# Two transfers on GpSimd's queue instead of six on ScalarE's, and half of the output weights loaded behind a store

## The chip, the cores and the metric

The kernel runs on one core of a Trainium2 chip. A core has TensorE (PE) for matmuls, VectorE (DVE), ScalarE (ACT), GpSimd (POOL) and SyncE (SP), which here does nothing but request transfers. All engines run at once and wait for each other by semaphores. ScalarE and GpSimd can request transfers as well; a request stands in that engine's own instruction stream, so what comes behind it waits until it is issued. The metric is device time in microseconds of one execution: the median of several runs.

## The reference

One encoder layer is applied to two sequences, a prompt of 256 positions and a sample of 2048, with 1024 features each:

```python
h = rms_norm(x, g_pre)
q, k, v, z_a, u_f, z_f = split(h @ w_in)                # each 512 wide
y_a = neighbourhood_attention(q, k, v, rpb)             # 8 heads of 64, windows of 8 x 16 on a grid 64 wide
spec = jnp.fft.fft2(u_f as [s, 8, 64], axes=(s, 64), norm='ortho')
y_f = spec.real.reshape(s, 512) @ w_f + b_f             # a Fourier mix, then a dense product
mixed = concat([rms_norm(y_a, g_na) * silu(z_a), rms_norm(y_f, g_f) * silu(z_f)])
out = x + rms_norm(mixed @ w_out, g_post)
```

Everything is float32 from input to output. The kernel keeps that precision by splitting each operand of the large products into a rounded high part and a remainder (`h`, `l`) and summing three products (`mm3`, lines 160 to 162).

## The kernel before

The work runs in four stretches on TensorE.

First (0 to about 549 us) come the six input projections, with the sums of a fast matrix scheme made by VectorE and GpSimd. The results go to memory outside the core: `qD`, `kD`, `vD`, `zD` and, for the Fourier half, `ZD` (first stage of the transform over positions). In the same stretch the output weights are scaled and split, and stored as `woD` (`wo_split`, line 704).

Second (549 to 576 us) comes the second stage of the Fourier transform. It loops over four groups `gq` and five blocks of features `c` (`stage2`, line 1031). Each block's product lands in a PSUM tile (`pab`; in group 0 also `pny`, in group 2 also `pup` for the prompt), and ScalarE's rounded copy (`split_ps`, line 1012) and VectorE's difference (line 1013) put the parts into `abh`, `abl`. Block 4 holds one feature per group of 64, the thirty-third: a real transform over 64 features has 33 distinct terms, and the last of them has no room in the four full blocks. It is kept in `a32`, three copies of 32 partitions each: rounded, rounded, remainder.

Between groups, `pq` (line 1052) multiplies the cosine and sine tables `cs2` by the dense weights `wf`. It runs with `m = 1` behind group 1 and with `m = 0` behind group 2. For `m = 1`, every thirty-second row of the product belongs to that thirty-third feature. It is copied out (`nq_`), and four rows of each `c` are moved to the rows they have in `w32`, the partner of `a32`: partitions 0 to 31 rounded, 32 to 63 remainder, 64 to 95 rounded. One matmul of 96 rows (line 1265) thus does all three products of that feature. The moving across partitions is done by transfers through the zeroed tile `nw`: three on ScalarE's queue for each `c`, one to each copy. Then one ScalarE copy of 96 partitions and one VectorE subtraction on the middle 32 finish `w32`.

Third (576 to 613 us), for each of four blocks `e` of 128 output features, three column tiles `ti` (in the order 2, 0, 1) are multiplied (`y_mm`, line 1254) into PSUM tiles `py1` (ring "a") and `py2` (ring "b", two tiles), and put together (`y_out`, line 1268): ScalarE writes `t1` from `py1` with the bias, VectorE adds or subtracts `py2` into `Y`. `Y` has two buffers; block `e` writes the buffer of block `e - 2`. When a block is done its 256 prompt positions are stored (line 1304) and then its 2048 sample positions, 1 MB (line 1327). For the first blocks ScalarE and GpSimd also sum the squares of Y (lines 1333 to 1341). The first output tile needs rows of all four blocks back from memory as `y0` (lines 1323, 1324, 1326), multiplied by `z` and split (lines 1350 to 1354).

Fourth (613 us to the end) come attention, in 36 groups, with the Fourier half of the output product (`f_mm`, line 1444, weights `wo1`) between them, and then the attention half.

`wo1` is eight tiles of 512 KB: `wo1[n][c]` for two halves `n` of the output columns and four blocks `c` of inner features. All eight are loaded in one loop (lines 1234 to 1237) on SP, behind the first loads of q, v, z and tables for attention. The half `n = 0` is first used by `f_mm(0)` and `n = 1` by `f_mm(1)`, the first and the second product of the fourth stretch. The tiles come from the pool of `gt`, whose buffers the second stretch used for `zg` and `d2`.

What sets the order of the work: TensorE's order is that of the code throughout. Of the other engines it is so up to line 972 and from line 1343, where `e` is 3. Between these lines, so in all that the diff touches, a planner orders ScalarE, VectorE, GpSimd and SP ahead of time by its own estimates: what stands first in the code goes first unless it is reckoned to be not ready, and then something later may go ahead. Once made, the order is fixed, and on the chip each engine's queue waits at its head.

Of the kernel before, what the change touches and what calls it, by code (L numbers as in the profile page):

```python
# [10 lines left out]
F32 = mybir.dt.float32  # L11
F32R = mybir.dt.float32r
AF = mybir.ActivationFunctionType
ALU = mybir.AluOpType
# [150 lines left out]
def build(tc, A, O):  # L165
    nc = tc.nc
# [60 lines left out]
    def gt(shape, dtype, name):  # L227
        return gp.tile(shape, dtype, tag="g", name=name)
# [485 lines left out]
    for c in range(3, 6):  # L714
# [7 lines left out]
        if c == 4:  # L722
# [5 lines left out]
            for k in range(KC):  # L728
                for t in range(2):
                    ts = slice(128 * t, 128 * t + 128)  # L730
                    nc.vector.scalar_tensor_tensor(out=xp[:, k, ts], in0=xs[t][:, k], scalar=gpre[:, k:k + 1],
                                                   in1=ivb[0][:, ts], op0=ALU.mult, op1=ALU.mult)
# [257 lines left out]
    sm = pg.enter_context(tc.tile_pool(name="smF", bufs=1))  # L990
# [1 line left out]
    nc.sync.dma_start(cs2, A["cs"])  # L992
    wf = sm.tile([128, 4, 512], F32, name="wf")
    nc.sync.dma_start(wf, A["wf"])
    nw = sm.tile([96, 512], F32, name="nw")
    nc.gpsimd.memset(nw, 0.0)
    f256 = sm.tile([128, 2, 258], F32, name="f256")
    nc.sync.dma_start(f256, A["f256"])
# [12 lines left out]
    def split_ps(dh, dl, src, vec=False):  # L1011
        nc.vector.tensor_copy(dh, src) if vec else nc.scalar.copy(dh, src)
        nc.vector.tensor_tensor(out=dl, in0=src, in1=dh.bitcast(F32), op=ALU.subtract)
# [36 lines left out]
    w32 = ab.tile([96, 512], F32R, name="w32")  # L1050

    def pq(m):
        h = gt([128, 2, 512], F32R, "pqh")
        l = gt([128, 2, 512], F32R, "pql")
        for c in range(2):
            p = ps.tile([128, 512], F32, tag="a", name="ppq")
            for x in range(2):
                nc.tensor.matmul(p[64 * x:64 * x + 64], cs2[:, m, :], wf[:, 2 * c + x, :], start=True, stop=True)
            if m == 0:
                split_ps(h[:, c], l[:, c], p)  # L1060
                continue
            nq_ = sm.tile([128, 512], F32, name="nq", bufs=2)
            nc.scalar.copy(nq_, p)
            for r in range(3):
                nc.scalar.dma_start(nw[32 * r + 16 * c:32 * r + 16 * c + 16:4], nq_[::32])
            nc.scalar.activation(h[:, c], p, AF.Copy, scale=dnyq[:, 2:3])
            nc.vector.scalar_tensor_tensor(out=l[:, c], in0=p, scalar=dnyq[:, 2:3], in1=h[:, c].bitcast(F32),
                                           op0=ALU.mult, op1=ALU.subtract)
        PQ[m] = h, l
        if m:  # L1070
            nc.scalar.copy(w32, nw)
            nc.vector.tensor_tensor(out=w32[32:64], in0=nw[32:64], in1=w32[32:64].bitcast(F32), op=ALU.subtract)

    for gq in range(4):
        for c in range(5):
            stage2(gq, zgs[gq], c)
        if gq in (1, 2):
            pq(2 - gq)
# [45 lines left out]
    def prep(g):  # L1124
        pr, ts = g["pr"], g["ts"]
        g["qh"] = jl.tile([128, 256], F32R, tag="qh", name="qh", bufs=4)
        g["ql"] = jl.tile([128, 256], F32R, tag="ql", name="ql", bufs=4)
        if g["R"] is None:
            q = qD[pr, :, ts].rearrange("p (b x) -> p b x", b=2)
        else:  # L1130
            sg, x = divmod(g["R"], 2)
            t0 = TP + 1024 * sg + 512 * g["hc"]
            q = qD[pr, :, t0:t0 + 512].rearrange("p (b x) -> p b x", b=2)[:, :, 128 * x:128 * x + 128]
        nc.sync.dma_start(g["ql"].bitcast(F32).rearrange("p (b x) -> p b x", b=2), q)
# [25 lines left out]
    def split_q(g):  # L1160
        qh, ql = g["qh"], g["ql"]
        nc.scalar.copy(qh, ql.bitcast(F32))
        nc.gpsimd.tensor_tensor(out=ql, in0=ql.bitcast(F32), in1=qh.bitcast(F32), op=ALU.subtract)
# [48 lines left out]
    def soft(g, b):  # L1212
        m = g["m"][b]
        nc.vector.reciprocal(m[:, 4:6], m[:, 2:4])  # L1214
        for h in range(2):
            w = g["w"][b][:, h, :g["nr"] * g["t"][b][1]]
            nc.gpsimd.tensor_scalar(w, w, m[:, 4 + h:5 + h], 1.0, ALU.mult, ALU.mult)  # L1217
# [13 lines left out]
        prep_v(g)  # L1231
    load_t(0, 1)
    wo1 = [[gt([128, 2, 512], F32R, "wo1") for c in range(4)] for n in range(2)]
    for n in range(2):
        for c in range(4):
            nc.sync.dma_start(wo1[n][c].bitcast(F32),
                              woD[1, :, c, :, n * 512:n * 512 + 512].rearrange("x p d -> p x d"))
    prep(G[2])
    prep(G[3])
    for g in G[:2]:  # L1240
# [2 lines left out]
    sm = pg.enter_context(tc.tile_pool(name="smY", bufs=2))  # L1243
    sqy = pq_.enter_context(tc.tile_pool(name="sqy", bufs=1, side="right"))
    y0 = sqy.tile([128, 2, 4, 128], F32, name="y0")
    for t, (g, x) in enumerate(zip(G, (0, 640))):
        g["w"] = []
        for c0, w in g["t"]:
            n = 2 * g["nr"] * w
# [4 lines left out]
    def y_mm(e, ti):  # L1254
        n = 386 if ti == 2 else 384
        cs = slice(384 * ti, 384 * ti + n)
        p1 = ps.tile([128, 512], F32, tag="a", name="py1")
        p2 = ps.tile([128, 512], F32, tag="b", name="py2", bufs=2)
        es_ = slice(e * 128, e * 128 + 128)
        for m, p in ((0, p1), (1, p2)):  # L1260
            for c in range(2):
                mm3(nc, p[:, :n], PQ[m][0][:, c, es_], PQ[m][1][:, c, es_],
                    AB[m][0][:, c, cs], AB[m][1][:, c, cs], c == 0, m == 1 and c == 1)
            if m == int(e == 0 and ti == 2):
                nc.tensor.matmul(p1[:, :n], w32[:, es_], a32[:, cs], start=False, stop=True)
        return p1, p2, n
# [39 lines left out]
    def first_soft(g, f=None):  # L1306
        if f:
            for y in range(4):
                bias_max(g, *divmod(y, 2))
            f()  # L1310
        for y in range(4):
            if f is None:
                bias_max(g, *divmod(y, 2))
            exps(g, *divmod(y, 2))

    order = ExitStack()
    for e in range(4):
        Y = sqy.tile([128, T], F32, tag="Y", name="Y", bufs=2)
        if e < 3:
            for ti in (2, 0, 1):  # L1320
                y_out(e, ti, *y_mm(e, ti))
                if e == 2 and ti == 2:
                    nc.sync.dma_start(y0[:, 0, :3], yD[1, :3, :, :128].rearrange("c p t -> p c t"))
                    nc.sync.dma_start(y0[:, 1], zD[0, :, :128].rearrange("(c p) t -> p c t", p=128))
                if e == 2 and ti == 0:
                    nc.gpsimd.tensor_tensor(out=y0[:, 0, :3], in0=y0[:, 0, :3], in1=y0[:, 1, :3], op=ALU.mult)
            nc.sync.dma_start(yD[1, e, :, TP:], Y[:, TP:])
            if e == 2:
                Y2 = Y
            for i in range(T // SQ if e < 2 else 1):  # L1330
                ts = slice(i * SQ, i * SQ + SQ)
                if e == 0:
                    nc.scalar.activation(sqs[:, ts], Y[:, ts], AF.Square)
                elif e == 2:
                    sq = sm.tile([128, SQ], F32, tag="sqf", name="sqf", bufs=2)
                    nc.scalar.activation(sq[:, :TP], Y[:, :TP], AF.Square)
                    nc.gpsimd.tensor_tensor(out=sqs[:, :TP], in0=sqs[:, :TP], in1=sq[:, :TP], op=ALU.add)
                else:
                    sq = sm.tile([128, SQ], F32, tag="sqf", name="sqf", bufs=2)
                    nc.scalar.activation(sq, Y[:, ts], AF.Square)  # L1340
                    nc.gpsimd.tensor_tensor(out=sqs[:, ts], in0=sqs[:, ts], in1=sq, op=ALU.add)
            continue
        order.enter_context(tc.manual_schedule(engines=MAN))
        py = y_mm(e, 2)
        scores(G[0])
        first_soft(G[0], lambda: y_out(e, 2, *py))
        py = y_mm(e, 0)
        y0h = gt([128, 2, 4, 128], F32R, "y0h")
        y0h = [y0h[:, 0], y0h[:, 1]]
        nc.vector.tensor_tensor(out=y0[:, 0, 3], in0=Y[:, :128], in1=y0[:, 1, 3], op=ALU.mult)  # L1350
        sq = sm.tile([128, SQ], F32, tag="sqf", name="sqf", bufs=2)
        y_out(e, 0, *py, lambda: (nc.scalar.copy(y0h[0], y0[:, 0]),
                                  nc.scalar.activation(sq[:, :TP], Y[:, :TP], AF.Square)))
        nc.vector.tensor_tensor(out=y0h[1], in0=y0[:, 0], in1=y0h[0].bitcast(F32), op=ALU.subtract)
        soft(G[0], 0)
        soft(G[0], 1)

        nc.sync.dma_start(y0[:, 0], yD[1, :, :, 128:256].rearrange("c p t -> p c t"))
        nc.sync.dma_start(y0[:, 1], zD[0, :, 128:256].rearrange("(c p) t -> p c t", p=128))
        scores(G[1])  # L1360
        py = y_mm(e, 1)
        first_soft(G[1])
        nc.vector.tensor_tensor(out=sqs[:, :TP], in0=sqs[:, :TP], in1=sq[:, :TP], op=ALU.add)
        split_q(G[2])
        soft(G[1], 0)
        y_out(e, 1, *py)
# [6 lines left out]
    sm = pt.enter_context(tc.tile_pool(name="smA", bufs=2))  # L1373
# [412 lines left out]
```

## Time and profile before

| | |
|---|---|
| median of three runs | 972.06 us (969.88, 972.06, 975.32) |
| the profiled execution | 973.49 us, of which the span from the first to the last instruction is 971.4 us |
| mean granted clock of TensorE | 0.996 |
| TensorE busy | 957.9 us, 99% of the span |
| VectorE, ScalarE, GpSimd busy | 710.4, 497.0, 430.3 us |
| moved by transfers | 279.22 MB, 287 GB/s on average |

In the rows that follow, a line of a timeline gives the start and the duration in microseconds, the engine, the line of the kernel, the operation, the tile written and the tile read, the shape and how many instructions are merged into the row. A bracket at the end gives the idle time of that engine just before, and what ended it. SPq and ACTq are the streams of requested transfers of SP and ScalarE; their duration is that of the request with its wait in the queue, not of the transfer. Tile names are cut of their numbers: `w` with `nw` beside it is `w32`, `wo` from `woD` is `wo1`.

### The profile page before, as it was taken

What the parts mean: (1) busy time and instruction counts of PE and PEld (TensorE: products, weight loads), DVE (VectorE), ACT (ScalarE), POOL (GpSimd) and SP (SyncE); (2) the same over time, 40 slices, a digit from 0 to 9 for tenths busy, and PEclk for the clock granted to TensorE, in tenths of its full rate; (3) what the DMA queues carried; (4) which work ended last, traced back from release to release, by engine and by line L of the source; (5) the groups of instructions that cost most, each with busy time, mean ns of one, the idle gap of its engine ahead of it and who ended that gap; (6) DMA issues with size and microseconds to landing.
All of it is one profiled execution on the core that took longest, in us unless ns stands there. A gap on an engine that the chain in (4) does not pass through costs nothing. (4 is left out here: it accounts for less than half of the span.)

```text
span 971.4 us, 17021 instructions
## 1 busy us (share of the span) xinstructions
PE 957.9 (99%) x5737; PEld 799.2 (82%) x5737; DVE 710.4 (73%) x1306; ACT 497.0 (51%) x1080; POOL 430.3 (44%) x401
## 2 busy tenths in 40 slices
PE   9999999999999999999999999999999999999997
PEld 7889988888888888888888878888787888778886
DVE  6768988777986767797776454776765656649997
ACT  5836675433325533333344255677666676644443
POOL 3100003364752202756745033577677686524544
PEclk9999999999999999999999999999999999999999
DMA  9899696556849996599889897698877998979993
GB/s 333 306 373 356 235 364 239 193 193 258 318 157 381 347 408 240 210 374 331 304 301 335 303 307 298 188 284 288 264 230 235 288 296 279 287 250 340 339 340 127
DMA packets 146286, 279.22 MB, mean 287 GB/s; under 512 B 13738, under 2 KB 84096, under 8 KB 142808
## 3 DMA queue, kind: packets, MB, share of 16 engines
q1 hardware_dynamic: 145720, 277.69, 81.8%
q8 instruction: 46, 0.75, 0.3%
q10 hardware_dynamic: 480, 0.44, 0.2%
q14 instruction: 40, 0.33, 0.1%
HBM read 183.66 MB, written 101.52 MB: 294 GB/s over the span
## 5 line engine op out<-in xcount | busy, mean ns | idle before, releaser
L160 PE MATMUL mm<-xh,wa 128*128 128x512 f32 x448 | 174.4, 389 | 0.0
L161 PE MATMUL mm<-xl,wa 128*128 128x512 f32 x448 | 174.3, 389 | 0.0
L162 PE MATMUL mm<-xh,wa 128*128 128x512 f32 x448 | 174.3, 389 | 0.0
L532 POOL TENSOR_TENSOR ws<-wr 128x512 f32<-128x512 f32 x16 | 22.5, 1406 | 227.7 <-DMA wr<-wz 209.8
L1217 POOL TENSOR_SCALAR w<-w,m 128x465 f32<-128x465 f32 (+9 forms) x136 | 85.6, 643 | 43.6 <-DVE m L1214 33.5
L160 PEld LDWEIGHTS mm<-xh,wa 128*128 128x128 f32 x448 | 84.1, 188 | 17.7
L162 PEld LDWEIGHTS mm<-xh,wa 128*128 128x128 f32 x448 | 84.1, 188 | 17.5
L161 PEld LDWEIGHTS mm<-xl,wa 128*128 128x128 f32 x448 | 84.1, 188 | 17.3
L547 DVE TENSOR_TENSOR wa<-wr,wa 128x512 fp32r<-128x512 f32 x60 | 71.9, 1207 | 26.8 <-ACT wa L546 26.6
L1434 PE MATMUL po<-wo,yh 128*128 128x512 f32 x272 | 90.5, 414 | 0.0
L1434 PE MATMUL po<-w,yh 128*128 128x512 f32 x280 | 86.9, 391 | 0.0
L1210 ACT ACTIVATE w<-w,m 128x465 f32<-128x465 f32 (+9 forms) x136 | 78.3, 579 | 16.5 <-DVE m L1205 16.4
L1205 DVE CUSTOM_DVE_ANT_1 w<-s,tb 128x465 f32<-128x465 f32 (+8 forms) x124 | 61.2, 532 | 10.2 <-PE s L1183 9.3
L585 POOL TENSOR_TENSOR mt<-mt,rmask 128x880 f32<-128x880 f32 (+2 forms) x24 | 50.6, 2124 | 34.4 <-DVE mt L581 21.1
L161 PE MATMUL mm<-vl,xh 128*128 128x512 f32 x168 | 65.6, 390 | 0.2 <-DVE vl L478 0.2
L162 PE MATMUL mm<-vh,xl 128*128 128x512 f32 x168 | 65.4, 389 | 0.0
L160 PE MATMUL mm<-vh,xh 128*128 128x512 f32 x168 | 65.4, 389 | 0.0
L873 DVE TENSOR_TENSOR f<-u,mm 128x512 f32<-128x512 f32 x64 | 43.5, 679 | 26.2 <-PE mm L162 21.3
L1434 PEld LDWEIGHTS po<-w,yh 128*128 128x128 f32 x280 | 52.1, 188 | 11.2 <-issue 0.4
L546 ACT CAST wa<-wr 128x512 fp32r<-128x512 f32 x60 | 36.3, 617 | 44.5 <-PE mm L162 23.0
L1507 PE MATMUL ptb<-ident,w 128*120 128x128 f32 (+8 forms) x422 | 58.9, 277 | 0.1
L1511 DVE COPY pt<-ptb 120x384 f32<-120x384 f32 (+5 forms) x72 | 40.5, 563 | 25.1 <-PE ptb L1507 24.9
(265 smaller groups left out, 2400.8 us busy)
## 6 DMA issues: line engine op xcount, KB each, us to landing
wr<-wz SPq DMA_DIRECT2D x48, 512.0 KB
vl<-sD SPq DMA_DIRECT2D x20, 512.0 KB
xm<-xm SPq DMA_DIRECT2D x9, 1024.0 KB
oD<-ofs SPq DMA_DIRECT2D x18, 512.0 KB
of<-oD SPq DMA_DIRECT2D x18, 512.0 KB
yr<-yD SPq DMA_DIRECT2D x34, 256.0 KB
zD<-f SPq DMA_DIRECT2D x16, 512.0 KB
woD<-wo SPq DMA_DIRECT2D x16, 512.0 KB
```

The source lines that it names most:

```text
L160: nc.tensor.matmul(out, lh, rh, start=first, stop=False)
L161: nc.tensor.matmul(out, lh, rl, start=False, stop=False)
L162: nc.tensor.matmul(out, ll, rh, start=False, stop=last)
L547: nc.vector.tensor_tensor(out=o[:, 1], in0=src, in1=o[:, 0].bitcast(F32), op=ALU.subtract)
L585: nc.gpsimd.tensor_tensor(out=o, in0=i, in1=rmask[:, m0:m0 + n].unsqueeze(2).to_broadcast([128, n, 80]), op=ALU.add)
L873: nc.vector.tensor_tensor(out=dst(f, b), in0=src(uu[u]), in1=src(p), op=op)
L1205: nc.vector.tensor_tensor_reduce(out=rows(g["w"][b][:, h, :n], w), in0=rows(g["s"][2 * b + h][:, :nr * sw(w)], sw(w))[:, :, :w], in1=tv, s ...
L1210: nc.scalar.activation(w, w, AF.Exp, bias=m[:, h:h + 1], scale=-1.0, accum_out=m[:, 2 + h:3 + h])
L1217: nc.gpsimd.tensor_scalar(w, w, m[:, 4 + h:5 + h], 1.0, ALU.mult, ALU.mult)
L1434: nc.tensor.matmul(p, (d["l"] if x == 2 else d["h"])[:, c], w(n, int(x == 1), c), start=j == 0, stop=j == 11)
L1507: nc.tensor.transpose(ptb[h][:nk, j * 128:j * 128 + 128], g["w"][b][:, h, c0:c0 + nk], ident)
L1511: V.tensor_copy(o[:z, h, :n], ptb[h][:z, :n])
```

## The change

There are three edits. The tile `nw` shrinks from 96 to 32 partitions, with its memset. For each of the two `c`, one transfer requested by GpSimd takes the place of three requested by ScalarE. The three copies of `w32` are then made on chip: ScalarE copies `nw` to partitions 0 to 31 and again to 64 to 95, and VectorE subtracts the first copy from `nw` into partitions 32 to 63. Last, the loading of `wo1` becomes a function of `n`. Half 0 is loaded where all was loaded, and half 1 is requested in the code right behind the first block's large store of Y. The tiles of both halves are allotted at the old place.

```diff
-    nw = sm.tile([96, 512], F32, name="nw")
+    nw = sm.tile([32, 512], F32, name="nw")
     nc.gpsimd.memset(nw, 0.0)
...
             nc.scalar.copy(nq_, p)
-            for r in range(3):
-                nc.scalar.dma_start(nw[32 * r + 16 * c:32 * r + 16 * c + 16:4], nq_[::32])
+            nc.gpsimd.dma_start(nw[16 * c:16 * c + 16:4], nq_[::32])
             nc.scalar.activation(h[:, c], p, AF.Copy, scale=dnyq[:, 2:3])
...
         if m:
-            nc.scalar.copy(w32, nw)
-            nc.vector.tensor_tensor(out=w32[32:64], in0=nw[32:64], in1=w32[32:64].bitcast(F32), op=ALU.subtract)
+            for r in (0, 64):
+                nc.scalar.copy(w32[r:r + 32], nw)
+            nc.vector.tensor_tensor(out=w32[32:64], in0=nw, in1=w32[:32].bitcast(F32), op=ALU.subtract)
...
     wo1 = [[gt([128, 2, 512], F32R, "wo1") for c in range(4)] for n in range(2)]
-    for n in range(2):
+
+    def wo1_load(n):
         for c in range(4):
             nc.sync.dma_start(wo1[n][c].bitcast(F32),
                               woD[1, :, c, :, n * 512:n * 512 + 512].rearrange("x p d -> p x d"))
+
+    wo1_load(0)
     prep(G[2])
     prep(G[3])
...
             nc.sync.dma_start(yD[1, e, :, TP:], Y[:, TP:])
+            if e == 0:
+                wo1_load(1)
             if e == 2:
                 Y2 = Y
```

## The prediction

> **What bounds the kernel now.** I read the page's busy times first, then tables of the stages around the edit, then the timelines of each engine there, and last the queue of SP.
>
> ```profile
> PE   9999999999999999999999999999999999999997
> PE 957.9 (99%) x5737; PEld 799.2 (82%) x5737; DVE 710.4 (73%) x1306; ACT 497.0 (51%) x1080; POOL 430.3 (44%) x401
> 565.00:570.00 5.00, 4.28 (x56) 3.12 (x56) 3.46 (x8) 4.22 (x14) 1.91 (x2) 1.00 0.75 261
> ...
> 600.00:605.00 5.00, 5.00 (x31) 4.65 (x30) 2.14 (x16) 1.60 (x6) 1.01 (x1) 0.76 0.78 287
> ```
>
> TensorE is busy 99% of the span and every slice but the last is full, so the kernel is bound by the order of its matmuls: only a place where TensorE stands still or runs slowly is worth anything. The last two rows are each five microseconds out of a table of stretches (busy time and instructions per engine, then granted clock, DMA share, GB/s): from 600 the clock fell to 0.76 with TensorE busy throughout, and from 565 TensorE was idle for 0.72 us at full clock. These two places are what the edit touches.
>
> ```profile
> 595.65 0.34 PE L1265 MATMUL py<-a,w 96*128 96x384 f32 x1
> 597.96 0.41 PE L160 MATMUL py<-abh,pqh 128*128 128x384 f32 x1 [1.98 <-DVE Y L1278]
> ...
> 598.73 0.33 PE L161 MATMUL py<-abl,pqh 128*128 128x384 f32 x1
> 598.90 0.46 PE L162 MATMUL py<-abh,pql 128*128 128x384 f32 x1
> ...
> 602.38 0.34 PE L160 MATMUL py<-abh,pqh 128*128 128x386 f32 x1
> ```
>
> Stall A. Matmuls here start 0.175 us apart (598.73 to 598.90 shows it). From 595.65 to 597.96 are 2.31 us, so 2.13 are lost. One microsecond later the start-to-start distance nearly doubles; from 598.90 to 602.38 eleven matmuls take 3.48 us where 11 x 0.175 = 1.93 would do: 1.55 lost. Together 3.68 us. TensorE waited for VectorE's writes of Y, which free the PSUM tile that it needs next. Why were those late?
>
> ```profile
> 579.51 1.34 DVE L1278 TENSOR_TENSOR Y<-t,py 128x252 f32<-128x252 f32 x7 [2.26 <-ACT t L1270]
> 583.48 1.28 DVE L1278 TENSOR_TENSOR Y<-t,py 128x378 f32<-128x378 f32 x6 [1.17 <-PE py L162]
> 591.53 0.58 ACT L1270 ACTIVATE t<-py,bfs 128x386 f32<-128x386 f32 x1 [1.69 <-PE py L1265]
> 596.48 2.34 DVE L1278 TENSOR_TENSOR Y<-t,py 128x252 f32<-128x252 f32 x10 [4.89 <-DMA yD<-Y]
> 573.77 8.94 SPq L1236 DMA_DIRECT2D wo<-woD x8
> 583.27 1.85 SPq L1134 DMA_DIRECT2D ql<-qD x2
> 586.06 0.33 SPq L1304 DMA_DIRECT2D yD<-Y x1
> 587.40 0.33 SPq L1327 DMA_DIRECT2D yD<-Y x1
> 591.62 0.32 SPq L1327 DMA_DIRECT2D yD<-Y x1
> ```
>
> Y has two buffers. The third block of features (e = 2) writes the first block's buffer, and may do so only when that block's 1 MB store (issued 587.40) has landed, at 596.48. The data was ready at 583.48 + 1.28 = 584.76, but SP was still working off its queue: eight output-weight loads (8.94 us), two loads of q, the store of 256 positions whose data lay ready at 580.85. The store was issued 2.64 us after its data, behind 4 MB of weights.
>
> ```profile
> 560.43 0.59 ACT L1063 COPY nq<-ppq 128x512 f32<-128x512 f32 x1 [0.62 <-PE ppq L1058]
> 561.09 2.17 ACTq L1065 DMA_DIRECT2D nw<-nq x3
> 563.30 0.59 ACT L1063 COPY nq<-ppq 128x512 f32<-128x512 f32 x1 [1.70 <-DMA nw<-nq]
> 563.79 0.69 ACT L1066 ACTIVATE pqh<-ppq,dnyq 128x512 fp32r<-128x512 f32 x1
> 563.92 1.59 ACTq L1065 DMA_DIRECT2D nw<-nq x3
> 565.55 0.37 ACT L1012 CAST abh<-pab 128x256 fp32r<-128x256 f32 x1 [1.07 <-DMA nw<-nq]
> 564.51 0.75 DVE L1067 SCALAR_TENSOR_TENSOR pql<-ppq,dnyq,pqh 128x512 fp32r<-128x512 f32 x1 [2.12 <-ACT pqh L1066]
> 565.32 0.71 PE L1020 MATMUL pup<-f,up 128*128 128x129 f32 x4 [0.36 <-DVE pql L1067]
> 566.44 1.10 PE L1020 MATMUL pab<-d,zg 128*128 128x64 f32 x8 [0.41 <-DVE abl L1013]
> 567.77 0.62 ACT L1071 CAST w<-nw 96x512 fp32r<-96x512 f32 x1 [0.22 <-DMA nw<-nq]
> 568.48 1.71 DVE L1072 TENSOR_TENSOR w<-nw,w 32x512 fp32r<-32x512 f32 x1 [0.84 <-ACT w L1071]
> 570.91 1.08 PE L1058 MATMUL ppq<-wf,cs 128*64 128x512 f32 x4 [0.70 <-DVE abl L1013]
> ```
>
> Stalls B. ScalarE issues six small transfers of the thirty-third rows itself, 2.17 + 1.59 us in which its next instruction waits (ACTq is its queue). Its copy of the second half comes 1.70 us late, the chain copy, cast, VectorE's difference ends at 565.26, and TensorE stops 0.36 and 0.41 us: 0.77. Later VectorE's 1.71 us of w32 stands ahead of a difference whose PSUM tile TensorE wants: 0.70.
>
> **The change part by part.** The sum is against the profiled execution, 973.49 us.
>
> Moved weight loads. Nothing is added: the same eight loads. Behind the first block's store stand only four of them, half of 8.94 us, so SP is through them at 573.77 + 4.47 = 578.24, through q by 580.1, and the two stores can go when VectorE has written them, 580.85 and 584.76. If the large one still takes what it takes now, 587.40 to 596.48 = 9.08 us, it lands at 593.84; VectorE could begin when ScalarE's t is there, 591.53 + 0.58 = 592.11. That bound leaves it waiting 1.73 us; it needs 2.34 us and TensorE wants the tile at 595.65 + 0.175 = 595.83, so TensorE would stop 593.84 + 2.34 - 595.83 = 0.35. So short a stop should not cost clock: the gaps at 565 to 570 left it at 1.00. With 2 MB less ahead of it the store should be faster: I take no stop, gain 3.68, with 3.33 as the poor end.
>
> What is moved past. Behind the moved loads stand on SP the second block's store (591.62) and all that follows. Four issues from about 585.1 end at 589.6, before 591.62: no delay of issue, but 2 MB now lie ahead of that store on the way to memory. The fourth block writes that buffer:
>
> ```profile
> 604.60 1.33 DVE L1278 TENSOR_TENSOR Y<-t,py 128x252 f32<-128x252 f32 x7
> 598.22 0.43 SPq L1324 DMA_DIRECT2D y<-zD x1
> 599.66 0.37 SPq L1323 DMA_DIRECT2D y<-yD x1
> 603.04 1.01 POOL L1326 TENSOR_TENSOR y<-y 128x384 f32<-128x384 f32 x1 [3.89 <-DMA y<-yD]
> 606.22 0.62 ACT L1352 CAST y0h<-y 128x512 fp32r<-128x512 f32 x1
> 609.75 2.92 PE L1434 MATMUL po<-wo,y0h 128*128 128x512 f32 x12
> 613.86 3.02 PE L1434 MATMUL po<-wo,y0h 128*128 128x512 f32 x12
> ```
>
> If all is 4.45 us earlier, that write comes at 600.15, 8.5 us after the store's issue; now a store behind 2 to 4 MB took 9.08. So up to 0.6 us of wait for VectorE there. The PSUM tile that this write frees at 604.60 + 1.33 = 605.93 is wanted by the last six matmuls before 609.75, from 608.7: 2.8 us of room hide it. The rows for the first output tile (load 599.66, product 603.04, cast 606.22) have 606.22 - 604.05 = 2.17 us of room now, and shrink it if only TensorE gets faster; the first product needs y0h at 609.75, three microseconds after the cast. The moved half of the weights is first used at 613.86; issued by 589.6, it has over 20 us. All covered, 0.
>
> Transfers from GpSimd. Removed: six issues on ScalarE. Added: two on GpSimd, which has nothing to do until a table arrives, and the change leaves that table's transfer alone:
>
> ```profile
> 562.15 0.33 SPq L1104 DMA_DIRECT2D tb<-tp x1
> 568.09 1.56 POOL L1112 TENSOR_TENSOR tb<-cm,tb 128x640 f32<-128x640 f32 x1 [17.54 <-DMA tb<-tp]
> 578.51 0.34 PE L1265 MATMUL py<-a,w 96*128 96x386 f32 x1
> ```
>
> Behind GpSimd's two waits for nq stand only that table's mask and the splits of k after it; its 17.54 idle us hide any issue of up to some 5 us. ScalarE now goes copy (560.43, 0.59), cast, copy, cast (0.69): the second cast ends near 562.8 instead of 564.48, VectorE's difference near 563.6, ahead of 565.32 - 0.36 = 564.96, where TensorE wants the tile. The 0.77 go. No row shows a GpSimd transfer, so its landing is bounded by the nearest rows. The second nq lies ready at about 562.2. Soonest, as ScalarE's last three, whose issue ended at 565.51 and whose data was taken at 567.77: 2.26 us, at 564.5. Slowest, as the table, 562.15 to 568.09: 5.94, at 568.1. I take 3.85 (563.92 to 567.77), at 566.1, because those are the same rows to the same place.
>
> On-chip spread. One cast of 0.62 becomes two of 32 partitions; a row of 128 partitions (copy, 0.59) and one of 96 (0.62) hardly differ, so +0.62 of ScalarE, which the 3.76 us of removed issues more than cover. VectorE's difference is unchanged, 1.71, or less if it comes before GpSimd's mask at 568.09, beside which it ran. w32 is first used at 578.51, eight microseconds later. If the rows land at 566.1 the 0.70 stall may go too; at 568.1 ScalarE, free from about 565.2 by my estimate, waits 2.9 in the copy of w32; the casts behind it hold TensorE's PSUM tiles, and after one more block's products (1.10 + 0.71 = 1.81) it stops too: 1.1 us are lost. So B is between 0.77 + 0.70 = 1.47 and 0.77 - 1.1 = -0.3. I take +0.77, the part that hangs on ScalarE's own issues alone. The smaller memset lies in 17 idle us: 0.
>
> Sum: 3.68 + 0.77 = 4.45; 973.49 - 4.45 = 969.0 us. The profiled run is 1.43 above the median of 972.06, close to the 1.55 of the slow stretch: an estimate is that a usual run hasn't got it. Then the gain is 2.13 + 0.77 = 2.90 from 972.06, 969.2: the same time.
>
> The Trainium skill ("TensorE: Matmul & The Clock Gate", section "Part 1: The HAM clock gate") has the clock halved after at least one idle window of about 3.4 us. The rows differ: 2.13 us of idling were enough here, though the half-rate stretch of 3.48 is that window's length. By its rule the idle time alone would be gained, as in the first rival.
>
> **The rivals.**
>
> The slow pace is not the idle time's doing. Then the 1.55 stays: 973.49 - 2.90 = 970.6. For it: the idle was short. Against: the clock column, 0.76 right behind it. 0.05. This is also what the skill's rule gives.
>
> The loads don't move. The order of SP, ScalarE, VectorE and GpSimd here is a planner's, not the code's: the load of z (598.22) went ahead of the load of y (599.66), which the code has first. Loads that need nothing could be drawn ahead of a store that must wait. Then A stays: 973.49 - 0.77 = 972.7. Against: with a queue full, code order held; q (583.27) needed nothing and yet went after all eight. 0.12.
>
> Late rows, a little. Landing at 568.1: 973.49 - 3.68 + 0.3 = 970.1. 0.10.
>
> Slower: late rows, a lot. GpSimd makes its transfers slowly, ScalarE stands in the copy of w32 from 565.2, and TensorE stops 1.81 us later; a gap of two microseconds or more costs another 1.55. To be slower than the median by 0.5%, 976.9, TensorE has to lose 976.9 - 969.8 = 7.1, so 5.55 of waiting, a landing after 565.2 + 1.81 + 5.55 = 572.6, ten microseconds after the second nq. At 576 it is 973.49 - 3.68 + 8.99 + 1.55 = 980.4. Against: no transfer in these rows took that long. For: nothing shows GpSimd issuing one. 0.11. The Trainium skill ("SBUF — State Buffer", section "SBUF: two separate sides", the box on the "DVE blocks DMA" trap) says that VectorE's two-port operations keep GpSimd from writing descriptors, 620 ns becoming 3100. No run here shows it; VectorE's rows at 560 to 566 read PSUM.
>
> All of it. The 0.70 goes too: 5.15. From the median, where a run may have its slow stretch elsewhere, 972.06 - 5.15 = 966.9. 0.18.
>
> **How the numbers follow.** My forecast has 0.44. Half a percent, 4.86 us, is about what a measurement of this kernel can tell from no change (its three runs span 969.88 to 975.32). Below 967.2 only the last case ends: 0.18. Within it forecast, clock, no move, a little late: 0.44 + 0.05 + 0.12 + 0.10 = 0.71. Slower 0.11. The range reaches from 966.5, under the last case, to 973.5, over the unmoved loads with the spread of runs, and leaves out the slow case and little else.
>
> **What would show it.** A right: SP issues four weight loads, two stores, then four loads; VectorE's writes for the third block carry no wait for a store; the clock stays at 1.00 from 595 to 605. B right: no ScalarE wait on its own transfers, PE rows at the third and fourth block of the third group without idle time. Wrong: a ScalarE wait of several microseconds before the copies of w32, PE idle there, or a wait for the second store at the fourth block.

## The result and the profile after

The changed kernel takes 975.12 us (median of 22 runs, 968.99 to 980.19); the kernel before, run beside it 22 times, 970.9. The ratio is 1.0043, with a 95% interval of 1.0024 to 1.0062: a little slower, where a gain was forecast. The times fall in two groups. Ten runs took 968.99 to 974.22 (median 971.3) with a mean granted clock of 0.995 to 0.999, twelve 975.07 to 980.19 (median 978.15) with 0.989 to 0.993. Half the runs lose nearly 7 us that the others keep. The profiled run, 980.19 us with a span of 978.4, is of the second group.

First TensorE's own timeline. These rows of the kernel before mark its stages and were not shown yet.

```profile
559.30 1.94 PE L1058 MATMUL ppq<-wf,cs 128*64 128x512 f32 x8
569.13 1.08 PE L1058 MATMUL ppq<-wf,cs 128*64 128x512 f32 x4
571.92 4.44 PE L1020 MATMUL pab<-d,zg 128*128 128x64 f32 x56
576.29 0.45 PE L160 MATMUL py<-abh,pqh 128*128 128x386 f32 x1
...
579.04 0.34 PE L162 MATMUL py<-abh,pql 128*128 128x384 f32 x1
...
616.81 1.09 PE L1523 MATMUL pv<-pt,v 80*64 80x128 f32 x16
```

The same timeline of the changed kernel (lines 1065 to 1070 are one lower there, those from 1235 on one to five higher), with the rows that answer to those of the prediction:

```profile
561.38 1.94 PE L1058 MATMUL ppq<-wf,cs 128*64 128x512 f32 x8
569.97 1.08 PE L1058 MATMUL ppq<-wf,cs 128*64 128x512 f32 x4
573.21 1.43 PE L1058 MATMUL ppq<-wf,cs 128*64 128x512 f32 x4 [2.17 <-DVE abl L1013]
574.58 8.10 PE L1020 MATMUL pab<-d,zg 128*128 128x64 f32 x56
582.61 0.69 PE L160 MATMUL py<-abh,pqh 128*128 128x386 f32 x1
...
587.54 0.33 PE L162 MATMUL py<-abh,pql 128*128 128x384 f32 x1
...
614.52 3.29 PE L1439 MATMUL po<-wo,y0h 128*128 128x512 f32 x12
619.08 0.39 PE L1512 MATMUL ptb<-ident,kh 128*80 128x128 f32 x2 [0.49 <-POOL ql L1163]
620.47 0.39 PE L1512 MATMUL ptb<-ident,kh 128*80 128x128 f32 x2 [1.00 <-DVE pt L1516]
620.61 4.59 PE L1439 MATMUL po<-wo,y0h 128*128 128x512 f32 x12
625.13 1.09 PE L1528 MATMUL pv<-pt,v 80*64 80x128 f32 x16
```

Read the two side by side as a lag. At the product with `m = 1`, ahead of all that the edit touches but the memset, it is 561.38 - 559.30 = 2.08 us; the first stretch varies that much from run to run (the same product starts at 558.83 in a run shown below). At the next product it is 569.97 - 569.13 = 0.84. The 2.17 us stop ends at 573.21, 2.30 behind the 570.91 of before: by then the edit has cost 0.2 us. Then 56 matmuls take 8.10 us that took 4.44, and the third stretch starts 6.32 late. Stall A is gone, no row of Y's stage has an idle time, and at the first output product the lag is down to 614.52 - 609.75 = 4.77. Two stops behind that product, 0.49 and 1.00 us, and a second product of 4.59 us instead of 3.02 bring it to 625.13 - 616.81 = 8.32. At the end it is 978.4 - 971.4 = 7.0.

So there are two new losses, one per edit. The table of stretches shows the first one's larger half:

```profile
565.00:570.00 5.00, 5.00 (x73) 4.71 (x71) 2.44 (x7) 2.12 (x7) 0.98 (x2) 1.00 1.03 406
570.00:575.00 5.00, 2.83 (x12) 0.79 (x11) 3.78 (x6) 4.14 (x10) 4.04 (x4) 0.88 0.68 178
575.00:580.00 5.00, 5.00 (x26) 5.00 (x25) 1.54 (x3) 1.59 (x5) 1.37 (x2) 0.50 0.97 325
...
600.00:605.00 5.00, 5.00 (x30) 5.00 (x30) 2.08 (x11) 3.42 (x9) 3.93 (x6) 1.00 1.06 391
...
620.00:625.00 5.00, 4.53 (x14) 3.32 (x14) 2.94 (x9) 1.34 (x4) 2.26 (x3) 0.66 0.51 210
```

From 565 to 570 TensorE is now fully busy (4.28 before) and from 600 the clock is 1.00 (0.76 before): both places named in the prediction are mended. But behind the one stop the clock is 0.50, with TensorE 100% busy, and from 620, behind the two stops of the second loss, it is 0.66: that is why the second product takes 4.59 us. Why does TensorE stop the first time? The timelines of GpSimd, ScalarE and VectorE:

```profile
563.71 1.32 POOL L1064 DMA_DIRECT2D nw<-nq  x2 [11.09 <-ACT pqh L1065]
570.43 1.52 POOL L1112 TENSOR_TENSOR tb<-cm,tb 128x640 f32<-128x640 f32 x1
570.02 1.26 ACT L1071 CAST w<-nw 32x512 fp32r<-32x512 f32 x2 [1.06 <-DMA nw<-nq]
570.67 1.83 DVE L1072 TENSOR_TENSOR w<-nw,w 32x512 fp32r<-32x512 f32 x1 [2.51 <-ACT w L1071]
```

ScalarE no longer spends 3.76 us on issues, and there it only comes sooner to a place where it must wait. The rows are taken at 570.02, 570.02 - 561.38 = 8.64 us after the product that makes them began; before it was 567.77 - 559.30 = 8.47. The two casts take 1.26 us (the one before took 0.62). VectorE's difference starts behind the first of them and takes 1.83 us, and only then, from 572.5, comes the difference that frees TensorE's tile. TensorE, freed of its two stops of 0.36 and 0.41, arrives 1.2 us earlier and waits for the same moment.

What sets that moment stands on GpSimd. Its mask of a table (line 1112) ends at 570.43 + 1.52 = 571.95, and VectorE's difference at 570.67 + 1.83 = 572.50, 0.55 us later. Before, the mask ended at 569.65 and the difference at 570.19, 0.54 later. In all ten profiles in which VectorE makes this difference it ends 0.53 to 0.55 us behind the mask, whenever it began. Counted from the start of the product with `m = 1`, the mask ends after 10.35 us before and 10.57 us now: that is the 0.2 us. ScalarE's next copy (`abh`) was done at 571.67, so without the mask TensorE's tile could have come free about 0.9 us sooner, by my estimate. No run moved the mask alone: that VectorE waits for it is read from these ten endings.

The second loss begins in the queue of SP, with the product on GpSimd and the cast on ScalarE that follow it:

```profile
593.33 0.33 SPq L1330 DMA_DIRECT2D yD<-Y  x1
593.71 3.44 SPq L1237 DMA_DIRECT2D wo<-woD  x4
600.16 0.33 SPq L1330 DMA_DIRECT2D yD<-Y  x1
602.49 0.32 SPq L1307 DMA_DIRECT2D yD<-Y  x1
...
608.47 0.37 SPq L1326 DMA_DIRECT2D y<-yD  x1
612.79 1.02 POOL L1329 TENSOR_TENSOR y<-y 128x384 f32<-128x384 f32 x1 [5.63 <-DMA y<-yD]
613.84 0.62 ACT L1357 CAST y0h<-y 128x512 fp32r<-128x512 f32 x1 [2.86 <-POOL y L1329]
```

The load of y reads what the third block's 128 KB store (602.49) writes, so it can only go when that has landed: 608.47, 6 us later. Before it went 599.66 - 597.85 = 1.8 us behind that store, whose row in SP's queue was

```profile
597.85 0.32 SPq L1304 DMA_DIRECT2D yD<-Y  x1
```

Issued in the 9.2 us ahead of the store are now 1 MB, 2 MB of weights and another 1 MB. ScalarE stands 2.86 us in the cast of y0h, with the exponentials of the first attention groups behind it, and TensorE waits for what its transposes need.

### The profile page after: what moved, and what is told of

It is laid out like the page before. It is cut to its first block, busy times and chain, and to the rows that moved or that the text cites. A ratio compares the mean times of both kernels' runs of the same rounds, so it can differ in the third digit from the quotient of the medians.

```text
span 978.4 us, 17019 instructions
## 1 busy us (share of the span) xinstructions
PE 965.1 (99%) x5737; PEld 805.7 (82%) x5737; DVE 707.0 (72%) x1306; ACT 497.8 (51%) x1081; POOL 429.5 (44%) x403
```

## The experiments

Each time is the median of 8 to 12 runs, beside the kernel before on the same chip. The ratio and its 95% interval come from all runs of both kernels and can differ a little from the ratio of the two medians. The four sets of runs were made on four chips, so kernels of different sets are compared by their ratios.

**One edit at a time.** The moved weights alone, ScalarE's six requests as before:

> The kernel before with the output weights' second half moved behind Y's first store, and nothing else; the thirty-third rows are requested by ScalarE as before. Theory 1 (the rows that GpSimd requested land late, ScalarE stands in the copy of w32, TensorE stops 2.17 us and then runs at half clock): the stalls of the third group are those of before (0.36, 0.41, 0.70 us), the store's stall (2.13 us and 1.55 us of slow clock) is gone, the first output tile's rows come late and cost 1 to 3.5 us: 968 to 972 us, none of the runs near 980. Theory 2 (the moved weights are what costs, through the late rows of the first output tile): 973 to 976 us, slower than before by about 3 us.

```diff
-    for n in range(2):
+    def wo1_load(n):
         for c in range(4):
...
+    wo1_load(0)
...
             nc.sync.dma_start(yD[1, e, :, TP:], Y[:, TP:])
+            if e == 0:
+                wo1_load(1)
```

972.36 us; before, 970.82; ratio 1.0017 (1.0007 to 1.0027). GpSimd's two requests and the spread alone:

> The kernel before with GpSimd's two requests and the spread on chip, and nothing else; all eight weight loads stand where they stood. Theory 1: the stop of about 2 us in the third group and, in about half the runs, the half clock of some 6 us behind it are there; the store's stall stays unless TensorE's lateness hides it: 973 to 980 us, runs in two clusters some 6 us apart. Theory 2: the loss is the weights', so this is before less the 0.77 us of ScalarE's own issues: 969 to 971 us, as narrow as before.

```diff
-            for r in range(3):
-                nc.scalar.dma_start(nw[32 * r + 16 * c:32 * r + 16 * c + 16:4], nq_[::32])
+            nc.gpsimd.dma_start(nw[16 * c:16 * c + 16:4], nq_[::32])
...
+            for r in (0, 64):
+                nc.scalar.copy(w32[r:r + 32], nw)
```

973.77 us; ratio 1.0028 (1.0011 to 1.0044). Neither theory alone holds: each edit loses by itself, 1.5 and 2.95 us, and together (4.2) about the sum. Weights alone, TensorE's timeline around its second output product, and GpSimd's product:

```profile
606.71 1.02 POOL L1329 TENSOR_TENSOR y<-y 128x384 f32<-128x384 f32 x1 [6.32 <-DMA y<-yD]
608.43 3.29 PE L1439 MATMUL po<-wo,y0h 128*128 128x512 f32 x12 [0.53 <-ACT y0h L1357]
614.52 4.59 PE L1439 MATMUL po<-wo,y0h 128*128 128x512 f32 x12
619.04 1.09 PE L1528 MATMUL pv<-pt,v 80*64 80x128 f32 x16
```

The late y rows and the slow second product (4.59 us) are there without any change to the third group. GpSimd alone, TensorE's stop and the stretches behind it:

```profile
572.79 1.08 PE L1058 MATMUL ppq<-wf,cs 128*64 128x512 f32 x4 [1.91 <-DVE abl L1013]
575.00:580.00 5.00, 5.00 (x58) 4.86 (x57) 2.35 (x6) 2.93 (x8) 3.39 (x4) 1.00 0.90 332
```

Here is the other group: this run of 971.0 us has the stop of 1.91 us and the clock stays at 1.00. Of its twelve runs, five took 969.61 to 971.0 or 973.89 at 0.997 to 0.999, seven 973.52 to 978.82 at 0.990 to 0.993. Stall A is gone from this run as well (TensorE is busy throughout from 595 to 600, at 1.00): it comes to Y's stage at 578.17, 1.88 us later than in the profile of before, and doesn't stop for Y's store. So the two losses don't simply add up, and that their sum fits is in part chance.

**Who requests, and how many.** The changed kernel with ScalarE making the two requests (`nc.scalar.dma_start` for `nc.gpsimd.dma_start`):

> The changed kernel, but ScalarE requests the two transfers instead of GpSimd; the spread on chip stays. If GpSimd's requests are what is slow (1.32 us for two, taken 4.9 us after the last): the rows land 2.3 to 3.9 us after their issue as ScalarE's did before, the copies of w32 wait less than 1 us, TensorE stops under 1 us there, no half clock: 967 to 971 us with a narrow spread. If the rows are late because memory is busy, whoever asks: a wait of 3 us or more stays and the time is that of the changed kernel, 971 to 980 us.

973.81 us; ratio 1.0033 (1.0013 to 1.0052), two groups again. And GpSimd with three requests per half, straight to their places, one cast of 96 partitions as before:

> The changed kernel, but GpSimd requests three transfers per half as ScalarE did before, straight to their partitions, and one cast of 96 partitions follows. If GpSimd's requests are slow: six cost some 4 us of GpSimd instead of 1.32, the rows land later still, by 1 to 3 us, and the time is that of the changed kernel or worse, 975 to 982 us. If the spread (two casts, a difference that reads two places) is what costs: 969 to 972 us.

```diff
-            nc.gpsimd.dma_start(nw[16 * c:16 * c + 16:4], nq_[::32])
+            for r in range(3):
+                nc.gpsimd.dma_start(nw[32 * r + 16 * c:32 * r + 16 * c + 16:4], nq_[::32])
```

974.84 us; ratio 1.0043 (1.0029 to 1.0058). The start of the `m = 1` product and the cast of w32, ScalarE's two requests:

```profile
559.36 1.94 PE L1058 MATMUL ppq<-wf,cs 128*64 128x512 f32 x8
567.88 1.26 ACT L1071 CAST w<-nw 32x512 fp32r<-32x512 f32 x2 [1.49 <-DMA nw<-nq]
```

GpSimd's six, with TensorE's stop and the stretch behind it:

```profile
558.83 1.94 PE L1058 MATMUL ppq<-wf,cs 128*64 128x512 f32 x8
561.16 3.55 POOL L1065 DMA_DIRECT2D nw<-nq  x6 [11.09 <-ACT pqh L1066]
570.74 0.62 ACT L1071 CAST w<-nw 96x512 fp32r<-96x512 f32 x1 [2.54 <-DMA nw<-nq]
574.00 1.76 PE L1020 MATMUL pab<-d,zg 128*128 128x64 f32 x32 [1.83 <-DVE abl L1013]
575.00:580.00 5.00, 5.00 (x41) 4.89 (x41) 0.85 (x2) 1.21 (x4) 0.72 (x1) 0.66 0.99 315
```

Two requests by ScalarE are taken 8.52 us after the product began, two by GpSimd 8.64, ScalarE's six of before 8.47 (in four other profiles 8.09 to 8.35, where the cast shows no wait for them). Which engine makes the two requests makes little difference to when the rows are there. GpSimd's six are taken after 11.91. What holds the rows is probably the full memory (DMA share 1.03 from 565 to 570 in the changed kernel), but no run emptied it.

**The changed kernel once more.**

> The changed kernel once more, unaltered, for the profile of another run and more times. Theory (the idle time before the third group's last product is in every run, and whether the clock is halved behind it is chance): TensorE waits 1.9 to 2.3 us for VectorE there whatever the time; the times fall in two clusters, about 969 to 974 with a mean clock of 0.995 or more and 975 to 980 with 0.993 or less, and if the profiled run is of the first, its clock stays at 1.00 from 570 to 590. Rival (the wait itself is short in some runs, because the rows land sooner): a fast profiled run shows a wait under 1 us there.

976.08 us; ratio 1.0044 (1.0027 to 1.0062): the same loss. Four runs took 970.74 to 975.37 us at a mean clock of 0.995 to 0.998, eight 975.73 to 979.99 at 0.988 to 0.993. The profiled run took 979.99 us and its stop 1.98 us, so the rival isn't answered.

**Each loss mended.** The kernel before with the second half behind the load of y:

> The kernel before (ScalarE requests the rows) with the weights' second half loaded behind the load of the first output tile's y rows, pinned there. If e1 lost its gain because the second half and the big stores stood ahead of that tile's 128 KB store (landing 6.1 us after its issue): the store's stall (3.7 us) stays gone, y's rows are multiplied within 4 us of that store's issue, y0h is cast without a wait of 3 us, no stop at the second output product: 967 to 969 us. If that chain is late for another reason (Y's writes simply come when they come), the stop of about 2.4 us and the slow clock behind it stay: 971 to 973 us. If the weights now come too late for the second product, a wait of TensorE for the load of wo shows it: 972 us and more.

```diff
+                    y_ld = nc.sync.dma_start(y0[:, 0, :3], yD[1, :3, :, :128].rearrange("c p t -> p c t"))
...
+                    with tc.issue_after(y_ld.ins):
+                        wo1_load(1)
```

971.34 us; before, 971.6; ratio 0.9991 (0.9976 to 1.0007), no change clear of the spread. GpSimd's product and TensorE's next stop:

```profile
601.71 1.02 POOL L1331 TENSOR_TENSOR y<-y 128x384 f32<-128x384 f32 x1 [1.57 <-DMA y<-yD]
618.80 0.73 PE L1439 MATMUL po<-wo,yh 128*128 128x512 f32 x2 [1.51 <-ACT ofs L1468]
```

The first tile's rows come in time and its stop is gone, so the weights ahead of the small store were its cause. But now 2 MB and a 1 MB store stand ahead of the fourth block's 128 KB store, which the second output tile reads (the store is issued at 603.70, the load can go at 612.22), and that tile stops instead. GpSimd making w32:

> The kernel before with GpSimd's two requests and the spread on chip, but GpSimd also makes the two casts and the difference of w32; the eight weight loads stand where they stood. Theory (what stops TensorE is that ScalarE stands in the cast of w32 and VectorE in its difference, with TensorE's PSUM tiles behind them): no idle time of TensorE from 560 to 575, clock 1.00 there, 1.0 to 1.5 us better than the kernel before and no second cluster: 969 to 971 us, or up to 3 us more if TensorE's earliness gives the wait for Y's store its whole length. Rival (GpSimd's requests disturb by themselves, or memory does): 973 to 975 us as with GpSimd's requests alone.

```diff
             for r in (0, 64):
-                nc.scalar.copy(w32[r:r + 32], nw)
-            nc.vector.tensor_tensor(out=w32[32:64], in0=nw, in1=w32[:32].bitcast(F32), op=ALU.subtract)
+                nc.gpsimd.tensor_copy(w32[r:r + 32], nw)
+            nc.gpsimd.tensor_tensor(out=w32[32:64], in0=nw, in1=w32[:32].bitcast(F32), op=ALU.subtract)
```

971.32 us; ratio 0.9997 (0.9981 to 1.0012): the time of before. GpSimd's difference, and the only row of TensorE with a wait from 549 to 640:

```profile
570.88 1.26 POOL L1072 TENSOR_TENSOR w<-nw,w 32x512 fp32r<-32x512 f32 x1
598.16 0.66 PE L160 MATMUL py<-abh,pqh 128*128 128x384 f32 x1 [2.89 <-DVE Y L1278]
```

All three stops of the third group are gone. The first two go wherever ScalarE's six requests go, as the changed kernel shows; the last goes here, so ScalarE and VectorE standing at w32 were its cause. GpSimd's mask comes behind w32 here, at 576.34, so the run doesn't part the casts from the mask. TensorE comes earlier to Y's store and waits there 2.89 us, with the clock at 0.76 and 0.90 in the two stretches from 595 to 605: what was won is lost again. Both mends:

> The changed kernel with both mends: GpSimd also makes w32, and the weights' second half goes behind the load of the first output tile's y rows. If the two losses are these two and nothing else: none of the four stalls (0.36, 0.41, 0.70 and 2.13 us), none of the two new ones, clock 1.00 from 549 to 625: 3.7 + 1.5 us below the kernel before at most, 965 to 968 us, narrow. If something else is late in their place: 969 to 972 us.

970.41 us; before, 971.6; ratio 0.9981 (0.9966 to 0.9997), better than both kernels and short of 965 to 968. GpSimd's product for the second output tile waits for its loads (that of z stands behind that of y in SP's queue), the same late store as with the mended weights alone (issued at 601.67, the load of y goes at 610.67), and TensorE stops 1.98 us:

```profile
614.67 1.27 POOL L1416 TENSOR_TENSOR y<-y 128x512 f32<-128x512 f32 x1 [6.03 <-DMA y<-zD]
```

**Where else the weights can go.** In the kernel with both mends memory has room ahead of 600 (the last column but one of its table of stretches, 0.45), so the second half went earlier:

```profile
595.00:600.00 5.00, 5.00 (x36) 4.67 (x35) 3.04 (x14) 2.74 (x7) 3.12 (x5) 1.00 0.45 129
```

> GpSimd makes w32 as in the kernel with both mends, and the weights' second half goes one step earlier: behind the first block's store of 256 positions, ahead of its 1 MB store. Theory (in the kernel with both mends the second half and the third block's store, both ahead of the fourth block's 128 KB store, delayed the second output tile's rows by 9 us, and memory had room from 585 to 600): nothing of the weights is left on the way after 593, both y chains come in time, Y's 1 MB store lands near 593 and VectorE waits for it about 2 us without stopping TensorE: clock 1.00 from 549 to 625, no TensorE idle time over 0.5 us there, 965 to 968 us. Rival (2 MB ahead of the store bring its stall back): a stop of 1 to 3 us in the third block and half clock behind it, 969 to 972 us.

> As the kernel before it in this list, but the second half is divided: two loads ahead of Y's 1 MB store and two behind it. Theory: the store lands 2.5 us sooner than with four ahead, VectorE waits under 1 us for it, and the two loads behind it are done by 595, ahead of the third block's 128 KB store: 965 to 968 us. Rival (any weights behind Y's first store reach into the first tile's rows): a wait of GpSimd of 4 us or more for the y rows, stop at the second output product, 970 to 972 us.

> The kernel before with ScalarE's six requests as they were, and only the weights' second half moved to behind the first block's 128 KB store, ahead of the 1 MB store. Theory: the stalls of the third group stay (1.47 us together, clock 1.00), the store's stall of 2.13 and 1.55 us is gone or under 0.5 us, the y chains come in time: 967 to 970 us. Rival (the order of loads and store makes no difference as memory must carry all of it anyway): 970 to 972 us as before.

The edits to `y_out`, behind the store of 256 positions; the second is the divided one, whose other two loads follow the 1 MB store (and whose third 1 MB store is pinned behind the load of y):

```diff
             nc.sync.dma_start(yD[1, e, :, :TP], Y[:, :TP])
+            if e == 0:
+                wo1_load(1)
...
+            if e == 0:
+                wo1_load(1, (0, 1))
```

All four ahead of the 1 MB store: 971.69 us; before, 970.55; ratio 1.0001 (0.9985 to 1.0017). Divided: 969.13 us, ratio 0.9982 (0.9968 to 0.9997). Four ahead with ScalarE's requests of before: 971.07, ratio 1.0008 (0.9998 to 1.0018). The rows of each, in this order; in the second, VectorE's wait for the store and TensorE's only one:

```profile
596.96 0.41 PE L160 MATMUL py<-abh,pqh 128*128 128x384 f32 x1 [1.39 <-DVE Y L1281]
```

```profile
592.42 1.34 DVE L1281 TENSOR_TENSOR Y<-t,py 128x252 f32<-128x252 f32 x7 [2.07 <-DMA yD<-Y]
609.41 0.39 PE L1515 MATMUL ptb<-ident,kh 128*80 128x128 f32 x2 [0.59 <-DVE pt L1519]
```

```profile
596.48 0.41 PE L160 MATMUL py<-abh,pqh 128*128 128x384 f32 x1 [0.44 <-DVE Y L1281]
```

With 2 MB ahead of the store its stall is back (1.39 us, though the clock stays at 1.00): VectorE's write begins 595.47 - 586.05 = 9.42 us behind the store's issue, 9.08 before. With 1 MB ahead VectorE waits 2.07 us, TensorE doesn't, and of the late y rows a stop of 0.59 us is left. By the ratio the divided kernel and the one with both mends (0.9982 and 0.9981) are the fastest, 0.2% under the kernel before, and both stay above their 965 to 968. As the divided kernel also has the pinned store, what the division alone is worth isn't shown. The last one's smaller stop, 0.44 us in this profile, shows no gain in its times. From the product with `m = 1` to `pv` it takes 613.76 - 559.40 = 54.36 us, 0.71 less than the kernel before in the profile shown next (614.74 - 559.67 = 55.07). That is little beside the spread of its runs, 969.74 to 972.93; why not even that shows stays open.

**How large was the stall that was to go?** The kernel before, profiled again:

> The kernel before, unaltered, for the profile of another run: the prediction's largest term, 3.68 us of the store's stall, was read from one run of 973.5 us, 2.6 above the median of 970.9 that more runs gave. If the stall is in every run, a profile of 970 to 971 us still shows TensorE waiting about 2 us for VectorE's write of Y in the third block, with or without the slow clock behind it. If the stall depends on the run, the profile shows under 1 us there and the clock at 1.00 from 595 to 610; then most runs had little to win, and the gain of the moved weights was mis-sized by 2 to 3.7 us.

970.99 us; the profiled run took 970.12. TensorE around the old stop, and the stretch behind it:

```profile
595.83 0.34 PE L1265 MATMUL py<-a,w 96*128 96x384 f32 x1
597.45 0.41 PE L160 MATMUL py<-abh,pqh 128*128 128x384 f32 x1 [1.28 <-DVE Y L1278]
600.00:605.00 5.00, 5.00 (x41) 4.42 (x42) 3.21 (x20) 3.66 (x12) 1.02 (x1) 1.00 0.74 274
```

The stall is there, but 597.45 - 595.83 - 0.175 = 1.45 us long, and the clock stays at 1.00.

## Why the prediction was wrong

**Stall A: right in kind, too large.** SP did issue four loads, the stores, then four loads, no write of Y waits for a store, and the clock is 1.00 from 595 to 605. The lag falls from 6.32 at the start of Y's stage, and another 8.50 - 6.32 = 2.18 of slow clock later (587.54 against 579.04), to 4.77: 3.73 us are won, the 3.68 of the sum. But the sum measured it in one run. In the run of 970.12 us it is 1.45. The prediction saw that the 1.55 might not be usual, and not that the 2.13 might not be either.

**Stalls B: the step "what of it lies on the path" failed.** "I take +0.77": the two stops did go, and 1.2 us were won up to 569.97 (the 0.77 are idle times, the rest is lost around them). All of it came back at the next row, since its start was set by w32, not by ScalarE's issues: by the rows, taken at 570.02, the casts, and the end of GpSimd's mask, behind which VectorE's difference ended. The prediction saw the mask beside that difference and drew from it only that the difference might take less. It took a landing of 3.85 us after nq and set the slow end, a landing at 568.1, aside with 0.10. On the time of before the rows were taken at 570.02 - 2.08 = 567.94, the slow end. For it the working gave -0.3 in place of +0.77, and the 0.2 us lost are close to that in number; the mask is no part of that working. How late GpSimd itself would be was no part of it: its two requests took 1.32 us, six 3.55, some 0.6 each, and the blocking of these requests that the prediction cites from the Trainium skill's "SBUF — State Buffer" is in no run here.

**The clock behind that stop: left out of the term.** This is the largest miss. The prediction knew that 2.13 us of idling had cost clock at stall A, charged 1.55 for it in the rival with very late rows, and nothing in the rival with slightly late ones (970.1), though the 1.1 us that it counted there and the 0.70 that it left standing make 1.8; in the run they came as one stop of 2.17. The measured price is not 1.55: 14.33 us (573.21 to 587.54) stand for 8.13 (570.91 to 579.04), 6.2 us, in about half the runs. The difference between the groups' medians is 6.9, and their clocks fit it: 0.997 against 0.991 over 978 us make 5.9. Twelve of 22 runs with 6.2 us make 3.4 on average, of the 4.2 us by which the changed kernel is slower; the first group's 971.3 is nearly the time of before. No profile of the changed kernel is of the first group: that its clock stays up behind the stop is read from these clocks and from the run of GpSimd's requests alone.

**The rows of the first output tile: "All covered, 0" failed.** The prediction counted issue times and SP's queue, and for memory only the wait of the write that follows the second block's store. It did not follow the third block's 128 KB store, which the load of y needs: it was issued behind 4 MB, and the 2.17 us of room were not enough for 4 more. From the first output product to `pv` the changed kernel takes 625.13 - 614.52 = 10.61 us, and so does the kernel with the weights alone (619.04 - 608.43), against 7.06 before: 3.55 lost, the size of all that stall A gave. Of these, 1.49 are the two stops and 4.59 - 3.02 = 1.57 the slow clock behind them.

**The moved half itself and SP's order** were right: the weights are never waited for, and the loads moved.

The Trainium skill ("TensorE: Matmul & The Clock Gate", section "Part 1: The HAM clock gate") names an idle window of about 3.4 us for the clock to fall and says that the windows run freely, so that the same kernel can differ from run to run. The two groups agree with the second; the first does not hold to the letter, as 1.98 and 2.17 us of idling were enough in two runs and 1.91 was not in another. Nor does it fit the second loss: behind 0.49 and 1.00 us, parted by two small matmuls, the clock fell in all five profiles that have this pair (to 0.66 in the stretch shown).

## What to carry to other kernels

Taking work off an engine wins only if nothing else holds the next step: before a wait is counted as gained, ask what the engine will then wait for, and follow transferred data to the time it is used. Several short stops can be cheaper than one long one, since a long one can halve TensorE's clock, and what that costs depends on the work behind it; but they must lie apart: 0.36, 0.41 and 0.70 us spread over 6 us left the clock at 1.00, 0.49 and 1.00 us close together did not. Where an instruction's time varies from run to run, look at what ran beside it and ended just before it. A load or store that is moved delays every later small transfer that goes to memory and comes back, so follow each such chain, not only the queue that requests it.

## What the runs showed that was not expected

The half clock lasts longer behind some work than behind other. In the changed kernel it began within 1.4 us of the stop's end and held through all 56 small matmuls (128x64, 8.10 us, TensorE 100% busy) until 587.5, nearly 5 us into Y's products (128x386 and 128x384). With GpSimd's six requests the stop came later, Y's products began 1.7 us behind its end, and the stretch from 575 to 580 at 0.66 is all that was slow; at stall A, also among Y's products, it was 1.55 us. The Trainium skill ("TensorE: Matmul & The Clock Gate", section "Part 1: The HAM clock gate") asks for about 3.4 us of sustained work for the clock to return; that fits the products of Y and not the small matmuls, which kept TensorE busy without bringing it back. They do keep a clock that is up: before, the same 56 ran 4.44 us at 1.00. That small matmuls don't bring the clock back is argued from these three places, and not tested.

VectorE's difference of 32 partitions took 0.75 to 2.06 us in ten profiles, the shortest with GpSimd's six requests. Its length goes by when it began, and its end is always 0.53 to 0.55 us behind GpSimd's mask: there it began 0.20 us ahead of the mask's end, in the others 1.02 to 1.52. So most of its time looks like waiting for an engine with which it shares no data. GpSimd, given the same difference, needed 1.26 us, and stood in a queue that nobody waited for.
